# Rolling an 8192 x 8192 array by 100 columns: heads through SBUF, or unaligned pieces straight from HBM to HBM

## The chip, the cores and the metric

The kernel runs on one core of a Trainium2 chip. The metric is the device time of one execution in microseconds; the figure is the median of several runs. Array rows are 8192 float32 values, so a row is 32,768 bytes, and a column is 4 bytes. Input and output both lie in HBM, 268.4 MB each.

## The reference

```python
def setup_inputs():
    return {
        "x": np.random.randn(8192, 8192).astype(np.float32),
        "shift": 100,
    }

def reference(x: np.ndarray, shift: int) -> np.ndarray:
    return np.roll(x, shift, axis=1)
```

Nothing is calculated. Each row of the output is the same row of the input moved right by s = 100 columns, and the last 100 columns of the input become the first 100 of the output (the wrapped end, 400 bytes a row).

## The kernel before

The kernel cuts each output row at column a. For s = 100 the first two lines below make a = 256, so the cut is at byte 1024 of the row.

```python
s = shift % n_cols
a = -(-s // 128) * 128
if 0 < a <= 384 and a + 128 <= n_cols:
    a += 128
g = a - s                      # 156
engines = [nc.sync, nc.scalar]
```

**The long pieces**, output columns 256 to 8191, come from input columns 156 to 8091. They are copied straight from HBM to HBM. A block is 64 rows; each of its four DMAs takes 16 rows (every fourth one), and the DMAs alternate between the queues of SP (`nc.sync`) and ACT (`nc.scalar`). In the last four of the 128 blocks every DMA is cut into two halves of the row.

```python
xm = x.rearrange("(c e j) w -> c j e w", e=16, j=4)
om = out.rearrange("(c e j) w -> c j e w", e=16, j=4)
blocks = n_rows // 64
mid = (a + n_cols) // 256 * 128
for c in range(blocks):
    parts = ((a, mid), (mid, n_cols)) if c >= blocks - 4 and a < mid else ((a, n_cols),)
    for j in range(4):
        for lo, hi in parts:
            engines[j % 2].dma_start(out=om[c, j, :, lo:hi], in_=xm[c, j, :, lo - s:hi - s])
```

**The heads**, output columns 0 to 255, consist of the wrapped end (100 columns) and the first 156 columns of the input row. They go through SBUF on GpSimd's own queue, in four stages of 2048 rows. For three rows of four one load reads 256 columns that begin 100 columns ahead of the row's start in memory, so that the end of the row above and the start of this row come as one piece; the vector engine copies the two parts to their rows in the tile `h`. Then four stores for each stage write 1024 bytes a row.

```python
Q, J = 4, 4
n_st = n_rows // (P * Q * J)                       # 4 stages
for k in range(n_st):
    t = reads.tile([P, Q - 1, J, a], x.dtype)
    h = heads.tile([P, Q, J, a], x.dtype)
    for q in range(1, Q):
        lead = bass.AP(tensor=x.tensor, offset=(k * P * J * Q + q) * n_cols - s, ...)
        nc.gpsimd.dma_start(out=t[:, q - 1], in_=lead)
    nc.gpsimd.dma_start(out=h[:, Q - 1, :, :s], in_=xt[k, Q - 1, :, :, n_cols - s:])
    nc.vector.tensor_copy(h[:, :Q - 1, :, :s], t[:, :, :, :s])
    if g > 0:
        nc.gpsimd.dma_start(out=h[:, 0, :, s:], in_=xt[k, 0, :, :, :g])
        nc.vector.tensor_copy(h[:, 1:, :, s:], t[:, :, :, s:])
    tiles.append(h)
for k, h in enumerate(tiles):
    for q in range(Q):
        nc.gpsimd.dma_start(out=ot[k, q, :, :, :a], in_=h[:, q])
```

Of the kernel before, what the change touches and what calls it, by code (L numbers as in the profile page):

```python
# [1 line left out]

# [4 lines left out]


@with_exitstack
def kernel(  # L10
    ctx: ExitStack,
    tc: tile.TileContext,
    x: bass.AP,
    shift: int,
    out: bass.AP,
):
    nc = tc.nc
    n_rows, n_cols = x.shape
    s = shift % n_cols
    a = -(-s // 128) * 128  # L20
    if 0 < a <= 384 and a + 128 <= n_cols:
        a += 128
    g = a - s
    P = nc.NUM_PARTITIONS
    engines = [nc.sync, nc.scalar]
    n_chunks = 16
    rows = n_rows // n_chunks

    xm = x.rearrange("(c e j) w -> c j e w", e=16, j=4)
    om = out.rearrange("(c e j) w -> c j e w", e=16, j=4)
    if a < n_cols:
        blocks = n_rows // 64
        mid = (a + n_cols) // 256 * 128
        for c in range(blocks):
            parts = ((a, mid), (mid, n_cols)) if c >= blocks - 4 and a < mid else ((a, n_cols),)  # L40
            for j in range(4):
                for lo, hi in parts:
                    engines[j % 2].dma_start(out=om[c, j, :, lo:hi], in_=xm[c, j, :, lo - s:hi - s])
    if a == 0:
        return


    if a > 512:
        for i in range(n_chunks):
            r = slice(i * rows, (i + 1) * rows)  # L50
            nc.gpsimd.dma_start(out=out[r, :s], in_=x[r, n_cols - s:])
            if g > 0:
                nc.gpsimd.dma_start(out=out[r, s:a], in_=x[r, :g])
        return

    Q, J = 4, 4  # L60
    n_st = n_rows // (P * Q * J)
    reads = ctx.enter_context(tc.tile_pool(name="reads", bufs=n_st))
    heads = ctx.enter_context(tc.tile_pool(name="heads", bufs=n_st))
    xt = x.rearrange("(k p j q) c -> k q p j c", q=Q, j=J, p=P)
    ot = out.rearrange("(k p j q) c -> k q p j c", q=Q, j=J, p=P)
    tiles = []
    for k in range(n_st):
        t = reads.tile([P, Q - 1, J, a], x.dtype)
        h = heads.tile([P, Q, J, a], x.dtype)
        for q in range(1, Q):  # L70
            lead = bass.AP(tensor=x.tensor, offset=(k * P * J * Q + q) * n_cols - s,
                           ap=[[J * Q * n_cols, P], [Q * n_cols, J], [1, a]])
            nc.gpsimd.dma_start(out=t[:, q - 1], in_=lead)  # L73
        nc.gpsimd.dma_start(out=h[:, Q - 1, :, :s], in_=xt[k, Q - 1, :, :, n_cols - s:])  # L74
        nc.vector.tensor_copy(h[:, :Q - 1, :, :s], t[:, :, :, :s])  # L75
        if g > 0:
            nc.gpsimd.dma_start(out=h[:, 0, :, s:], in_=xt[k, 0, :, :, :g])  # L77
            nc.vector.tensor_copy(h[:, 1:, :, s:], t[:, :, :, s:])  # L78
        tiles.append(h)
    for k, h in enumerate(tiles):  # L80
        for q in range(Q):
            nc.gpsimd.dma_start(out=ot[k, q, :, :, :a], in_=h[:, q])  # L82


# [1 line left out]
_INS = ['x', 'shift']  # L86
_OUTS = [((8192, 8192), 'float32')]

_NUMBERS = {'shift': 100}


# [26 lines left out]
```

## Time and profile before

| | |
|---|---|
| time, median of 3 | 829.27 us (829.12 to 830.45) |
| span of the profiled execution | 817.9 us |
| DMAs of long pieces | 496 of 496 KB, 32 of 248 KB |
| DMAs of heads on GpSimd's queue | 20 loads, 16 stores |
| vector engine, GpSimd busy | 7.7 us, 28.9 us |

Of the long pieces there are 248 DMAs of 496 KB on each of the two queues and, in the last four blocks, 16 of 248 KB on each. Among the profile's DMA queues q1 and q10 carry the long pieces of the two issuing engines, and q0 carries the heads. The MB of a queue count each packet once: a piece that goes from HBM to HBM is one packet, though it is read from HBM and written to it, and a head is two, one into SBUF and one out of it. A queue's share is the time its packets took out of the time of all 16 DMA engines. Besides data packets there are packets of 4 bytes that tell of a finished transfer; they take almost no time but are counted. The row "DMA" gives the busy share of the engines in 40 slices of the span, in tenths.

### The profile page before, as it was taken

What the parts mean: (1) busy time and instruction counts of PE and PEld (TensorE: products, weight loads), DVE (VectorE), ACT (ScalarE), POOL (GpSimd) and SP (SyncE); (2) the same over time, 40 slices, a digit from 0 to 9 for tenths busy, and PEclk for the clock granted to TensorE, in tenths of its full rate; (3) what the DMA queues carried; (4) which work ended last, traced back from release to release, by engine and by line L of the source; (5) the groups of instructions that cost most, each with busy time, mean ns of one, the idle gap of its engine ahead of it and who ended that gap; (6) DMA issues with size and microseconds to landing.
All of it is one profiled execution on the core that took longest, in us unless ns stands there. A gap on an engine that the chain in (4) does not pass through costs nothing. (4 is left out here: it accounts for less than half of the span.)

```text
span 817.9 us, 633 instructions
## 1 busy us (share of the span) xinstructions
DVE 7.7 (1%) x8; POOL 28.9 (4%) x40
## 2 busy tenths in 40 slices
DVE  0000000000000000000000000000000000000000
POOL 3000000010010000000000000000000000000000
DMA  9999999999999999999999999999999999999998
GB/s 307 333 348 342 347 355 347 355 356 344 350 338 363 359 351 354 361 346 360 334 333 341 326 335 331 331 332 337 328 338 331 330 336 331 335 334 326 331 308 299
DMA packets 21572, 276.89 MB, mean 339 GB/s; under 512 B 9024, under 2 KB 9024, under 8 KB 13120
## 3 DMA queue, kind: packets, MB, share of 16 engines
q10 hardware_dynamic: 8448, 130.04, 46.5%
q1 hardware_dynamic: 8448, 130.04, 45.9%
q0 software_dynamic: 4672, 16.78, 6.9%
q14 instruction: 4, 0.03, 0.0%
HBM read 268.44 MB, written 268.44 MB: 656 GB/s over the span
## 5 line engine op out<-in xcount | busy, mean ns | idle before, releaser
L82 POOL DMA_DIRECT2D out_dram<-h x16 | 13.2, 827 | 196.6 <-DMA out_dram<-h 112.1
L73 POOL DMA_DIRECT2D t<-in_x_dram x12 | 9.5, 795 | 60.4 <-DMA h<-in_x_dram 30.1
L75 DVE COPY h<-t 128x1200 f32<-128x1200 f32 x4 | 3.1, 785 | 233.6 <-DMA t<-in_x_dram 233.6
L78 DVE COPY h<-t 128x1872 f32<-128x1872 f32 x4 | 4.9, 1224 | 0.0
L74 POOL DMA_DIRECT2D h<-in_x_dram x4 | 3.0, 749 | 45.6 <-DMA t<-in_x_dram 45.6
L77 POOL DMA_DIRECT2D h<-in_x_dram x4 | 3.0, 751 | 42.8 <-DMA t<-in_x_dram 42.8
L99 POOL MEMSET const-float32-0.0<- 128x1 f32 x1 | 0.1, 100 | 0.2 <-issue 0.2
L99 POOL MEMSET const-bfloat16-1.0<- 128x1 bf16 x1 | 0.1, 103 | 0.0
L99 POOL MEMSET const-float32-1.0<- 128x1 f32 x1 | 0.1, 100 | 0.0
L99 POOL MEMSET const-uint8-127<- 128x1 uint8 x1 | 0.1, 100 | 0.0
## 6 DMA issues: line engine op xcount, KB each, us to landing
out_dram<-in_x_dram ACTq DMA_DIRECT2D x248, 496.0 KB, 12.7
out_dram<-in_x_dram SPq DMA_DIRECT2D x248, 496.0 KB, 12.7
out_dram<-h POOLq DMA_DIRECT2D x16, 512.0 KB, 112.6
t<-in_x_dram POOLq DMA_DIRECT2D x12, 512.0 KB, 95.4
out_dram<-in_x_dram SPq DMA_DIRECT2D x16, 248.0 KB, 5.7
out_dram<-in_x_dram ACTq DMA_DIRECT2D x16, 248.0 KB, 5.9
h<-in_x_dram POOLq DMA_DIRECT2D x4, 312.0 KB, 92.0
h<-in_x_dram POOLq DMA_DIRECT2D x4, 200.0 KB, 97.9
```

The costliest lines, as they stand in the source:

```text
L73: nc.gpsimd.dma_start(out=t[:, q - 1], in_=lead)
L74: nc.gpsimd.dma_start(out=h[:, Q - 1, :, :s], in_=xt[k, Q - 1, :, :, n_cols - s:])
L75: nc.vector.tensor_copy(h[:, :Q - 1, :, :s], t[:, :, :, :s])
L77: nc.gpsimd.dma_start(out=h[:, 0, :, s:], in_=xt[k, 0, :, :, :g])
L78: nc.vector.tensor_copy(h[:, 1:, :, s:], t[:, :, :, s:])
L82: nc.gpsimd.dma_start(out=ot[k, q, :, :, :a], in_=h[:, q])
L99: nc = _bacc.Bacc("TRN2", target_bir_lowering=False, num_devices=1)
```

## The change

The new kernel does away with the heads' detour. The long pieces start where the roll makes them start, at output column 100 (byte 400) and input column 0, and run to the row's end, 8092 columns or 32,368 bytes. The wrapped ends, 100 columns or 400 bytes a row, are copied from HBM to HBM as well, by one DMA for each block of 64 rows on ACT's queue, after the block's four long pieces. The last blocks are not cut in half. GpSimd, the vector engine and SBUF have no part in it any more. It is for a simpler path: all of the array is moved by the two hardware queues, with no second transfer and no waiting on tiles.

```diff
-    a = -(-s // 128) * 128
-    if 0 < a <= 384 and a + 128 <= n_cols:
-        a += 128
-    g = a - s
...
-    if a < n_cols:
-        blocks = n_rows // 64
-        mid = (a + n_cols) // 256 * 128
-        for c in range(blocks):
-            parts = ((a, mid), (mid, n_cols)) if c >= blocks - 4 and a < mid else ((a, n_cols),)
-            for j in range(4):
-                for lo, hi in parts:
-                    engines[j % 2].dma_start(out=om[c, j, :, lo:hi], in_=xm[c, j, :, lo - s:hi - s])
...
-    (heads: all loads, copies and stores shown above)
...
+    blocks = n_rows // 64
+    xb = x.rearrange("(c e j) w -> c j e w", e=16, j=4)
+    ob = out.rearrange("(c e j) w -> c j e w", e=16, j=4)
+    xw = x.rearrange("(c e j) w -> c e j w", e=16, j=4)
+    ow = out.rearrange("(c e j) w -> c e j w", e=16, j=4)
...
+    tail = 0
+    for c in range(blocks - tail):
+        for j in range(4):
+            engines[j % 2].dma_start(out=ob[c, j, :, s:], in_=xb[c, j, :, :n_cols - s])
+        if s > 0:
+            engines[1].dma_start(out=ow[c, :, :, :s], in_=xw[c, :, :, n_cols - s:])
+    if tail:
...                            (not reached: tail is 0)
```

More of the change, by code (lines that the diff above doesn't have):

```diff
@@ L19 @@
     s = shift % n_cols
-    a = -(-s // 128) * 128
-    if 0 < a <= 384 and a + 128 <= n_cols:
-        a += 128
-    g = a - s
-    P = nc.NUM_PARTITIONS
-    engines = [nc.sync, nc.scalar]
[L26 to L35, printed above, removed]
-    if a < n_cols:
-        blocks = n_rows // 64
-        mid = (a + n_cols) // 256 * 128
-        for c in range(blocks):
-            parts = ((a, mid), (mid, n_cols)) if c >= blocks - 4 and a < mid else ((a, n_cols),)
-            for j in range(4):
-                for lo, hi in parts:
-                    engines[j % 2].dma_start(out=om[c, j, :, lo:hi], in_=xm[c, j, :, lo - s:hi - s])
@@ L44 @@
[L44 to L79, printed above, removed]
@@ L80 @@
-    for k, h in enumerate(tiles):
-        for q in range(Q):
-            nc.gpsimd.dma_start(out=ot[k, q, :, :, :a], in_=h[:, q])
+    engines = [nc.sync, nc.scalar]
+    blocks = n_rows // 64
[3 more added lines that the diff above has]
+    ow = out.rearrange("(c e j) w -> c e j w", e=16, j=4)
+    xt = x.rearrange("(t c e j) w -> t j e c w", c=4, e=16, j=4)
+    ot = out.rearrange("(t c e j) w -> t j e c w", c=4, e=16, j=4)
@@ new lines @@
+    tail = 0
[5 more added lines that the diff above has]
+    if tail:
+        t = blocks // 4 - 1
+        if s > 0:
+            for c in range(blocks - tail, blocks):
+                engines[c % 2].dma_start(out=ow[c, :, :, :s], in_=xw[c, :, :, n_cols - s:])
+        for j in range(4):
+            engines[j % 2].dma_start(out=ot[t, j, :, :, s:], in_=xt[t, j, :, :, :n_cols - s])
```

## Prediction

> **What bounds the kernel now.** I read the page first: the DMA row and the byte counts, because no engine computes for more than 4% of the span.
>
> ```profile
> span 817.9 us, 633 instructions
> DVE 7.7 (1%) x8; POOL 28.9 (4%) x40
> ...
> DMA  9999999999999999999999999999999999999998
> ...
> q10 hardware_dynamic: 8448, 130.04, 46.5%
> q1 hardware_dynamic: 8448, 130.04, 45.9%
> q0 software_dynamic: 4672, 16.78, 6.9%
> ...
> HBM read 268.44 MB, written 268.44 MB: 656 GB/s over the span
> ```
>
> The 16 DMA engines are busy in every slice, and the three queues fill 46.5 + 45.9 + 6.9 = 99.3% of their time. HBM traffic is the least possible: the array is read once and written once. So the time is bytes over rate, plus a start and an end, and the question is what sets the rate. For that I compared two stretches of the DMA view: 40 to 300 us, where GpSimd's queue q0 runs beside the long pieces, and 380 to 780 us, where the long pieces run almost alone.
>
> ```profile
> q10 hardware_dynamic: 2520, 40.03, 43.1%
> q1 hardware_dynamic: 2517, 39.94, 42.2%
> q0 software_dynamic: 3107, 11.09, 15.0%
> ```
>
> ```profile
> q10 hardware_dynamic: 4160, 65.97, 50.2%
> q1 hardware_dynamic: 4165, 66.13, 48.9%
> q0 software_dynamic: 363, 1.31, 0.9%
> ```
>
> The columns are packets, MB and share of the engines' time. In the second stretch 132.1 MB of long pieces took 99.1% of 16 engines for 400 us, 6342 us of engine time: 20.8 bytes per ns, or 1.52 us for a row of 31,744 bytes. In the first, 79.97 MB took 85.3% of 16 x 260 us = 3548 us: 22.5 bytes per ns, 1.41 us for the same row. The same row is 8% faster when the engines also have SBUF work. So an engine's own speed isn't the limit. Now HBM traffic: a long piece is read from and written to HBM, a packet of q0 touches HBM once. First stretch: (2 x 79.97 + 11.09) MB in 260 us = 658 GB/s. Second: (2 x 132.1 + 1.31) in 400 us = 664 GB/s. The HBM traffic is nearly constant (1% apart) while the mix of work changes by 15 points. **My reading is that HBM traffic bounds the kernel at about 664 GB/s**, and that the SBUF detour of the heads costs only that 1% over the stretch in which it runs.
>
> Then the waits of the issuing queues and the end of the span:
>
> ```profile
> SPq L43 <- DMA out_dram<-in_x_dram: 671.1, 259, 3.9
> ```
>
> ```profile
> out_dram<-in_x_dram ACTq DMA_DIRECT2D x248, 496.0 KB, 12.7
> out_dram<-in_x_dram SPq DMA_DIRECT2D x248, 496.0 KB, 12.7
> ```
>
> ```profile
> 780.00:800.00 20.00, 0.00 (x0) 0.00 (x0) 1.00 0.89 299
> 800.00:818.00 18.00, 0.00 (x0) 0.00 (x0) 1.00 0.84 295
> ```
>
> SP issues 264 long pieces and waits for an earlier one before 259 of them. An issue takes 0.51 us, a transfer lands 12.7 us after it, and in 380 to 780 us each queue issued 131, one in 3.05 us. So 12.7 / 3.05, about four, are in flight on each queue, eight in all. The issuing engines are far from being the limit. The last fence (DMA share and GB/s are its last columns) is the stage with half rows: 16 DMAs of 248 KB on each queue. There the engines were busy for 0.89 and 0.84 and moved about 297 GB/s against 333. Over 38 us that is a loss of 38 x (1 - 297/333), about 4 us.
>
> [...] The wrapped ends are 400 B. No HBM write that short exists in the kernel before, so its trace can't say; 400 B pieces are only read there, into SBUF. [...] The long pieces before have an unaligned source (column 156, byte 624) and an aligned destination (byte 1024), and run at the rate above. After, it is the other way round: source byte 0, destination byte 400. [...]
>
> **The change, part by part.**
>
> Long pieces. 8192 rows of 8092 x 4 = 32,368 B, 265.2 MB instead of 260.0. With the heads, all 268.4 MB goes HBM to HBM. At the rate of the second stretch, (132.1 + 0.66) MB in 400 us or 332 GB/s of copying (q0's one-sided MB count half), this is 268.4 / 0.332 = 808 us. The page's own start costs little: the first 20 us ran at 304 GB/s, a loss of about 2 us.
>
> Removed: GpSimd's 36 DMAs and the DVE's 8 copies. DVE and POOL lie wholly beside the transfers, so their 7.7 and 28.9 us bring nothing. q0's HBM traffic isn't removed, it only moves. What is gained is the 1% (658 to 664) over the 380 us in which q0 was active: 380 x 0.9% = 3.4 us. That gain is already in the 808.
>
> Added: 128 head DMAs of 64 x 400 B. Each engine gets 4 pieces per DMA, 512 in all. Their bytes at 20.8 per ns are 19 ns a piece and are counted in the 808. What such a piece costs over its bytes isn't in this profile; I choose 20 to 60 ns as a guess, so 10 to 31 us of engine time. As HBM is the limit, most of this is hidden: before, q0 took 15% of engine time, of which about half was HBM-free, and the HBM rate fell by 1%, so some seven eighths of a loss of HBM demand was made up by the other engines. An eighth of 10 to 31 us is 1 to 4 us. [...] I take 6 us for the heads.
>
> ACT issues 256 + 128 DMAs of 0.52 us, 199 us of some 815: beside the path. The heads also take places among the eight in flight. A block is now four long pieces and one head, so of eight 6.4 are long: 6.4 x 1.55 is some 10 us of work queued on each engine instead of 12.4. With half rows it was some 6 us, and there the engines ran dry for 11 to 16%; at 10 us I expect hardly any of that, 1 us.
>
> The end. The stage of half rows, with its 4 us, goes. In its place the last whole rows drain with less evenness over engines: one row is 1.55 us, and a few rows of difference between engines would leave a similar 4 us.
>
> Sum of the span: 808 + 2 (start) + 6 (heads) + 1 (places in flight) + 4 (end), 821 us, against 817.9. The times of before lie 829.27 - 817.9 = 11.4 us above the span; I keep that: 832 us. As I hold both the 6 us and the end for cautious, I set the point at **830 us**: the change moves almost nothing, because HBM traffic stays as it was.
>
> **Rivals.**
>
> A. *Unaligned writes cost.* [...] A cost of 5% on the rate alone would give 830 + 40 = 870 us, and it could be more. For it: the kernel takes pains to start its long pieces at a multiple of 512 B and to write heads of 1024 B. Against: the same misalignment is there now on the read side[...]. I give it about one chance in six.
>
> B. *Short pieces block the engines.* [...] 100 ns or more a piece is 51 us of engine time, and if it is not hidden the time goes to some 850 to 870 us. For it: [...] the detour through SBUF, which avoids such pieces. [...]
>
> C. *Aligned reads help.* If the unaligned source now costs extra traffic and an unaligned destination does not, the rate rises by a few per cent: 800 to 812 us. For it: nothing in the profile[...]. One chance in twelve.
>
> D. *Heads are free and the end is smooth*: 808 + 2 + 3 + 11.4, about 824 us. This is the lower half of my range.
>
> **Range and chances.** A gain over 2% needs under 812.7 us, thus a span under 801 us and a copying rate above that of the quiet stretch; only C gives it: 0.09. A loss over 2% is above 845.9 us, which A or B bring: 0.29. Between lies 0.62. The range is 815 to 858 us: the lower end lies between C and D, the upper is a moderate A or B.
>
> **What would show it.** Right: in the changed profile HBM read and written stay at 268.44 MB, no q0 data, the copying rate in the middle is 328 to 336 GB/s, a long row takes 1.5 to 1.6 us of engine time, and a long piece lands in about 10 us. The heads' packets would take under 5% of the engines. A is right if long packets take clearly longer per byte than 1 / 20.8 ns with the DMA row full. B is right if the long ones keep their rate, ACT's queue takes clearly more time than SP's, or DMA shares fall. Slices below 0.95 in the middle would show that 6.4 places in flight are too few. I'd be wrong altogether if the bound isn't HBM traffic but a limit on each engine's packets: then fewer packets of q0 would show as a gain that I don't count.

## The result and the profile after

The kernel after takes **834.65 us** (median of 7), beside 829.42 us for the kernel before in the same runs: ratio **1.005, 95% interval 1.003 to 1.007**. The change is a small loss, clear of the noise. The prediction was 830 us, with a range of 815 to 858 us.

The page of the kernel after, the lines that answer to those shown of before:

```profile
span 829.0 us, 685 instructions
...
DMA  9999999999999999999999999999999999999998
GB/s 302 326 321 323 330 328 329 329 318 329 319 330 318 332 323 332 324 325 329 327 320 327 331 328 325 324 329 321 326 321 330 317 325 328 327 329 323 327 322 285
...
q10 hardware_dynamic: 18432, 135.88, 51.0%
q1 hardware_dynamic: 8192, 132.60, 48.2%
...
HBM read 268.44 MB, written 268.44 MB: 648 GB/s over the span
```

The engines are as full as before. The line of HBM bytes says less than the prediction hoped for. It gives 268,435,456 bytes each way, the size of the array to the byte, and for the kernel without heads (experiment 5) 265.16 MB, which is what its DMAs name. On these pages the line gives the bytes that the DMAs name; no run shows whether traffic beyond those would appear in it. q0 has gone. ACT's queue has 18,432 packets: 4096 long rows, 8192 heads and 6144 finish marks of 4 bytes, 16 for each of its 384 DMAs. So each 400 B piece is a packet of its own. A finish mark takes 9 ns in the mean; all 10,240 of both queues fill 5.8 us of an engine in the mean of the 16, 0.7% of the span. In the packet records the 8192 heads take 14.8 us of an engine in the mean, 1.8% of the span, which is most of the difference between 51.0% and 48.2%.

The first profile of before, span 817.9 us, is of an execution quicker than the timed ones. The kernel before, profiled again beside its timing runs, has a span of 826.4 us (experiment 1). Here is its DMA view from 380 to 780 us, then that of after (packets, MB, share of 16 engines; for the issues KB each and us to landing):

```profile
q10 hardware_dynamic: 4114, 65.31, 49.9%
q1 hardware_dynamic: 4117, 65.40, 48.9%
q0 software_dynamic: 480, 1.72, 1.1%
```

```profile
q10 hardware_dynamic: 8866, 65.39, 50.9%
q1 hardware_dynamic: 4007, 64.81, 48.8%
...
out_dram<-in_x_dram SPq DMA_DIRECT2D x126, 505.8 KB, 8.6
out_dram<-in_x_dram ACTq DMA_DIRECT2D x123, 505.8 KB, 10.8
out_dram<-in_x_dram ACTq DMA_DIRECT2D x62, 25.0 KB, 12.1
```

HBM traffic before: (2 x 130.71 + 1.72) MB in 400 us, 658 GB/s. After: 2 x 130.20 in 400 us, 651 GB/s. That is a rate 1% lower in the middle. From 40 to 300 us, where the detour was at work, the same views give 650 before and 652 after: there the new kernel is no slower. A queue's wait after:

```profile
SPq L31 <- DMA out_dram<-in_x_dram: 669.8, 207, 9.0
```

The longest single wait rose from 3.9 to 9.0 us. ACT's queue carries the heads as well, and SP's transfers land sooner (8.6 us against 10.8); that SP therefore runs ahead and waits longer is likely, but was not tested. It is no loss by itself: the DMA share stays at 0.99 to 1.01 from 40 to 780 us.

### The profile page after: what moved, and what is told of

Its sections match the earlier page's. It is cut to its first block, busy times and chain, and to the rows that moved or that the text cites. A ratio compares the mean times of both kernels' runs of the same rounds, so it can differ in the third digit from the quotient of the medians.

```text
span 829.0 us, 685 instructions
## 1 busy us (share of the span) xinstructions
POOL 0.2 (0%) x4
## 2 busy tenths in 40 slices
DMA packets 26629, 268.52 MB, mean 324 GB/s; under 512 B 18432, under 2 KB 18432, under 8 KB 18432
## 3 DMA queue, kind: packets, MB, share of 16 engines
q10 hardware_dynamic: 18432, 135.88, 51.0%
q1 hardware_dynamic: 8192, 132.60, 48.2%
HBM read 268.44 MB, written 268.44 MB: 648 GB/s over the span
## 6 DMA issues: line engine op xcount, KB each, us to landing
out_dram<-in_x_dram ACTq DMA_DIRECT2D x128, 25.0 KB, 12.1
```

## The experiments

Ratios are to the kernel before in the same set of runs. Four sets were run: experiments 1 to 4, 5 to 8, 9 to 11, and 12. They ran on different chips (numbers 4, 10, 11 and 10), and the kernel before took 829.3, 827.8, 819.4 and 829.4 us in them. So times of different sets are not compared, only ratios, on the assumption that a ratio carries over from chip to chip. Experiments 2 and 5 support it: 8064 columns took 0.9848 on chip 4, and by bytes 8092 columns should take 0.9882; on chip 10 they took 0.9886.

In the expectations, theory 1 is the prediction's reading that HBM traffic sets the time, theory 2 its rival A (unaligned writes cost), and theory B its rival B (each short piece holds an engine up). The 5% of rival A and the 100 ns a piece of rival B were suppositions of the author, not taken from a trace.

**1. The kernel before, once more** (no edit).

> The kernel before, unchanged, to have a span and a time of the same execution. The span of the first profile was 817.9 us while the executions took 829.4 in the median; after, span and time of one execution lie 1.8 us apart. If the first profile was just an unusually quick execution, this span is 825 to 830 us and time less span is about 2 us; the quiet stretch 380 to 780 us then shows 655 to 660 GB/s of HBM traffic instead of 664. If profile and time differ by a constant 11 us for this kernel, the span is again about 818.

Measured: 829.99 us, ratio 1.0001 (0.9986 to 1.0016). Span and time of the profiled execution: 826.4 and 828.55 us. Time is span plus some 2 us; the 11.4 us between the first profile and the timed runs was not a constant of the kernel. The spans of this kernel on chips 4 and 10 lie between 823.5 and 830.7 us, those on chip 11 between 815.8 and 820.3. Of these three the first profile's 817.9 us fits chip 11 alone; on which chip it was taken is not known.

**2 to 4. Alignment by itself.** The long pieces alone, 8064 columns, heads left out (the values of d and r for the first of the three). An offset is called aligned here if it is a multiple of 512 bytes, as the cuts of the kernel before are:

```diff
+    d, r, n = 100, 0, 8064
...
-            engines[j % 2].dma_start(out=ob[c, j, :, s:], in_=xb[c, j, :, :n_cols - s])
+            engines[j % 2].dma_start(out=ob[c, j, :, d:d + n], in_=xb[c, j, :, r:r + n])
-        if s > 0:
-            engines[1].dma_start(out=ow[c, :, :, :s], in_=xw[c, :, :, n_cols - s:])
```

With d = 100, r = 0 (destination unaligned):

> Only the long pieces, 8064 columns from input column 0 to output column 100 (destination unaligned, source aligned); the other 128 columns of a row are left out. Theory 1 (HBM traffic alone): 264.2 MB at the rate of the kernel after, about 815 to 820 us, and the same as the next two kernels within 0.5%. Theory 2 (unaligned writes cost): slower than the one with an aligned destination by over 1%.

With d = 128, r = 28 (source unaligned):

> The same 8064 columns, from input column 28 to output column 128: destination aligned to 512 bytes, source unaligned, the way of the kernel before; 128 columns left out. Theory 1: the same time as the one from column 0 to column 100 within 0.5%. Theory 2: faster than it by 1% or more. Theory 3 (unaligned reads cost): slower than it.

With d = r = 128 (both aligned, nothing shifted):

> The same 8064 columns, from input column 128 to output column 128: both aligned, so nothing is shifted; 128 columns left out. Theory 1: the same time as the other two within 0.5%. If alignment of either side costs, this is the fastest of the three, by the sum of both costs.

| destination, source | us | ratio, interval |
|---|---|---|
| byte 400, byte 0 | 818.33 | 0.9848, 0.9825 to 0.9871 |
| byte 512, byte 112 | 813.82 | 0.9799, 0.9776 to 0.9823 |
| byte 512, byte 512 | 810.08 | 0.9756, 0.9734 to 0.9778 |

Same bytes, same DMAs, and the executions of the three do not overlap (816.60 to 819.05, 812.37 to 815.82, 809.77 to 811.67 us). The unaligned source costs 3.7 us over the aligned copy, the unaligned destination 8.3 us. So turning the one into the other, as the change does, costs 4.5 us, 0.5%. Theory 1 in the form "only bytes count" misses this; theory 2 has the right sign, but its size (over 1%) is not reached; theory 3, that the kernel with the unaligned source is the slower of the two, falls. One offset of each kind was tried. The third kernel shifts nothing, so against it the distance between source and destination changes too; the 4.5 us between the first two is free of that, as both shift by 100 columns.

**5. The kernel after without heads.** Output columns 0 to 99 are left out:

```diff
-        if s > 0:
-            engines[1].dma_start(out=ow[c, :, :, :s], in_=xw[c, :, :, n_cols - s:])
```

> The kernel after without its 128 head DMAs: all else as it is, the first 100 columns of the output are left out. Its bytes are 3.28 MB fewer, about 10.0 us at the 326 GB/s of the middle of the kernel after. Theory 1 (heads cost their bytes and a few us more): 834.65 less 10 less 2 to 6, thus 819 to 823 us. Theory B (short pieces block the engines, 100 ns each): below 800 us. The two long-piece kernels that are known, 818.3 us for 8064 columns, speak for 821.

Measured: 817.9 us, ratio 0.9886 (0.9868 to 0.9904). The heads cost 1.005 - 0.9886 = 1.6% or about 13.6 us, with some 2 us of uncertainty. Their bytes are 10.0 us of it. Some 3.6 us, with the same 2 us of uncertainty, are left for their being short. Theory B, 100 ns a piece, falls. In the packet records an engine spends, in the mean of the 16, 802 us on long pieces and 14.8 us on heads in the kernel after, and 804 us on long pieces here: of the 14.8 us of the heads' packets 13.6 are paid.

**6. Half the HBM traffic.** The same long pieces, read from 128 rows in SBUF; the output is those rows over and over, heads left out:

```diff
+    pool = ctx.enter_context(tc.tile_pool(name="src", bufs=1))
+    src = pool.tile([128, n_cols], x.dtype)
+    nc.sync.dma_start(out=src[:], in_=x[0:128, :])
+    sv = src.rearrange("(e k) w -> k e w", k=8)
...
-            engines[j % 2].dma_start(out=ob[c, j, :, s:], in_=xb[c, j, :, :n_cols - s])
+            engines[j % 2].dma_start(out=ob[c, j, :, s:], in_=sv[(4 * c + j) % 8, :, :n_cols - s])
```

> The same long pieces of 32,368 bytes in the same DMAs on the same queues, but read from 128 rows held in SBUF instead of from HBM; heads left out, and the output holds the same 128 rows again and again. HBM is only written, so its traffic is halved while each DMA engine moves the same number of packets and bytes. Theory 1 (HBM traffic is the limit): the rate goes from 327 GB/s to that of the shortest long packet, 32,368 bytes in 1196 ns or 433 GB/s: a span near 615 to 650 us. Rival (each DMA engine is limited by its packets or by what it holds in flight, whatever HBM has to carry): 800 to 820 us, as without heads.

Measured: 692.26 us, ratio 0.837 (0.8353 to 0.8388). The view by stretches (start and end, length, POOL, clock, DMA share, GB/s):

```profile
40.00:100.00 60.00, 0.00 (x0) 1.00 1.00 276
100.00:160.00 60.00, 0.00 (x0) 1.00 1.00 331
160.00:220.00 60.00, 0.00 (x0) 1.00 1.00 414
220.00:400.00 180.00, 0.00 (x0) 1.00 1.01 429
400.00:640.00 240.00, 0.00 (x0) 1.00 1.00 423
```

From 220 us on the same engines, with packets of the same size in the same DMAs, carry 423 to 429 GB/s instead of the 327 of experiment 5. So the engines' own speed is not the limit of the copy from HBM to HBM; the limit lies on the side of HBM. The run doesn't tell HBM's bandwidth from the delay of its reads, as both are away, and reads of HBM alone were not run. One thing speaks against a fixed delay in each engine: in the packet records a long row of the kernel before takes 1.53 us in the mean when the heads are left out (experiment 8) and 1.48 us when they are there (experiment 1), although the heads then share the engines.

The total lies outside both expected ranges, because the first stretch is slow: 276 GB/s of writes alone, less than half of the 651 GB/s of HBM traffic in the kernel after, with the DMA share at 1.00. The amount of traffic can't explain that.

**7. Twice as many head pieces.** Same bytes and number of head DMAs, pieces of 200 B:

```diff
+    xh = x.rearrange("(d e j) w -> d e j w", e=16, j=8)
+    oh = out.rearrange("(d e j) w -> d e j w", e=16, j=8)
...
-        if s > 0:
-            engines[1].dma_start(out=ow[c, :, :, :s], in_=xw[c, :, :, n_cols - s:])
+        lo = c % 2 * (s // 2)
+        hi = lo + s // 2
+        engines[1].dma_start(out=oh[c // 2, :, :, lo:hi], in_=xh[c // 2, :, :, n_cols - s + lo:n_cols - s + hi])
```

> The kernel after, its heads in pieces of 200 bytes: 128 head DMAs as before, each with 128 rows and one half of the 100 columns, so the same bytes in twice as many pieces. Theory 1 (cost by bytes, the rest mostly hidden): 834 to 838 us. Theory B (cost by piece): the heads' cost above their bytes doubles; with 100 ns a piece that is 50 us more, with the 29 ns of a 400 B packet that the trace after shows at most 10 us more.

Measured: 840.59 us, ratio 1.0149 (1.0125 to 1.0172): 1% or some 8 us over the kernel after, with 2 to 3 us of uncertainty. The 834 to 838 of theory 1 is missed, and so is theory B with 100 ns a piece (50 us); the "at most 10 us" from the packets' own time holds. In the packet records a 400 B packet takes 24 ns in the median and 29 in the mean, a 200 B packet 16 and 19. For each of the 16 engines there are 512 packets of 29 ns after and 1024 of 19 ns here, so the packets themselves account for 4.6 us of the 8; the rest is at the edge of the uncertainty and not explained. At equal bytes, heads cost more when there are more of them.

**8. The kernel before without heads.** Only its long pieces, with half rows at the end; columns 0 to 255 are left out:

```diff
-    tiles = []
-    for k in range(n_st):
-        ...                        (all of the heads)
```

> The kernel before without its heads: only the long pieces, output columns 256 to 8191 with half rows in the last blocks; the first 256 columns are left out. Theory 1: 260.0 MB at 329 GB/s is 790 us, with 2 us of start and 4 of end 797 us; the detour through SBUF then costs 829.4 less 797, about 32 us for 16.8 MB of HBM traffic, of which 25 us are its bytes. If the detour were nearly as cheap as its HBM traffic alone: 804 us. If it took all its engine share (6.9% of 818, 56 us): 773 us.

Measured: 797.44 us, ratio 0.964 (0.962 to 0.9659). The detour costs 827.82 - 797.44 = 30.4 us, with some 2 us of uncertainty, as theory 1 said; 25.5 of them are the bytes at 329 GB/s. GpSimd's queue filled 6.9% of the engines' time, 56 us; little more than half of it is paid. The middle of the two kernels without heads, first this one, then experiment 5:

```profile
380.00:680.00 300.00, 0.00 (x0) 1.00 1.00 330
```

```profile
380.00:680.00 300.00, 0.00 (x0) 1.00 1.00 327
```

The last column, GB/s, differs by 0.7% before rounding (98.88 MB against 98.17), with the DMA share at 1.00 in both. That is near the 0.5% of alignment in experiments 2 to 4; the rows differ a little in length, too.

**9. The half rows put back** into the kernel after:

```diff
+    mid = n_cols // 2
...
+        parts = ((s, mid), (mid, n_cols)) if c >= blocks - 4 else ((s, n_cols),)
         for j in range(4):
-            engines[j % 2].dma_start(out=ob[c, j, :, s:], in_=xb[c, j, :, :n_cols - s])
+            for lo, hi in parts:
+                engines[j % 2].dma_start(out=ob[c, j, :, lo:hi], in_=xb[c, j, :, lo - s:hi - s])
```

> The kernel after with the long pieces of its last four blocks in halves again, as before had them. If the missing half rows cost something at the end, this gains 1 to 4 us over the kernel after (ratio 1.000 to 1.004 against 1.005); by the prediction, which put 4 us for either end, nothing changes (1.005).

Measured: ratio 1.006 (1.0047 to 1.0073), against 1.005 without them. The intervals overlap; half rows make no difference that these runs show. The ends by stretches, the kernel after first, then this one:

```profile
800.00:815.00 15.00, 0.00 (x0) 1.00 1.01 326
815.00:829.00 14.00, 0.00 (x0) 1.00 0.80 263
```

```profile
780.00:800.00 20.00, 0.00 (x0) 1.00 0.97 326
800.00:824.00 24.00, 0.00 (x0) 1.00 0.80 266
```

With whole rows the rate holds until 14 us before the end and then falls to 263; with half rows it is 266 over the last 24 us. Against 326 that is a loss of 14 x (1 - 263/326), about 3 us, and of 24 x (1 - 266/326), about 4 us.

**10. Heads issued by GpSimd**, whose DMAs the profile shows on a queue of their own (q0):

```diff
-        if s > 0:
-            engines[1].dma_start(out=ow[c, :, :, :s], in_=xw[c, :, :, n_cols - s:])
+        nc.gpsimd.dma_start(out=ow[c, :, :, :s], in_=xw[c, :, :, n_cols - s:])
```

> The kernel after with its head DMAs issued by GpSimd instead of ACT, the same pieces in the same order. They then take no place among the eight transfers of SP and ACT, and in the kernel before packets of GpSimd's queue joined ten or so 400 B pieces (4000 to 4400 bytes in some 160 to 170 ns, 16 ns a piece against 24 ns of a single 400 B packet after). Theory 1 (bytes): same as after, within 3 us (1.002 to 1.007). Rival (places in flight or the single packets cost what the heads cost above their bytes): 3 to 4 us less, about 1.000 to 1.001.

Measured: ratio 1.0027 (1.0013 to 1.0041), some 2 us better than on ACT, though the intervals overlap (1.003 to 1.007 on ACT). It falls inside the band given for theory 1 and short of the rival's. Its page has the heads in 2048 data packets of 1600 bytes:

```profile
q0 software_dynamic: 4096, 3.28, 2.2%
```

Here the queue joined four pieces to a packet (4096 packets less 2048 finish marks). In the kernel before it did the same with the heads on their way through SBUF: 16.78 MB in 4096 data packets, 4096 bytes each in the mean, so a head was not a packet of its own there. From 380 to 680 us 193 long pieces were issued, which land after 12.5 us: some eight of them in flight, by an estimate of 193 x 12.5 / 300. In the kernel after the view from 380 to 780 us gives, in the same way, some six ((126 x 8.6 + 123 x 10.8) / 400) and two heads (62 x 12.1 / 400). Whether the gain is from the two places or from the joined pieces isn't told apart. It is still no better than the kernel before.

**11. The kernel before, cut at column 128**: heads of 512 B through SBUF.

```diff
-    if 0 < a <= 384 and a + 128 <= n_cols:
-        a += 128
```

> The kernel before with the cut at column 128 instead of 256: heads of 512 bytes through SBUF, long pieces still aligned to 512 bytes and longer. The head detour carries half the HBM traffic. If what the detour costs above its bytes (30.4 less 25.5, about 5 us in the kernel before) goes with its bytes, this gains 2 to 3 us: ratio 0.997. If it goes with the number of pieces, which stays, the ratio is 1.000; if 512 B stores or 112 B loads are dear, over 1.003.

Measured: ratio 1.0041 (1.0026 to 1.0055), slower, as in the last of the three cases expected. The same long pieces alone, destination aligned and source at byte 112, stand at 0.9799 (experiment 3), so these heads cost 2.4%, 20 us, for 8.39 MB of HBM traffic whose bytes take 12.7 us at 330 GB/s: 7 us above the bytes, with 2 us of uncertainty, no less than the 4.9 us with pieces of 1024 B. Half the bytes in as many pieces do not halve the surplus. Which of the loads and stores it comes from was not tried.

**12. Neighbouring rows.** As experiment 10, but a long DMA takes 16 rows 32 KB apart instead of 128 KB:

```diff
-    xb = x.rearrange("(c e j) w -> c j e w", e=16, j=4)
-    ob = out.rearrange("(c e j) w -> c j e w", e=16, j=4)
+    xb = x.rearrange("(c j e) w -> c j e w", e=16, j=4)
+    ob = out.rearrange("(c j e) w -> c j e w", e=16, j=4)
```

> The kernel with head DMAs on GpSimd, its long pieces taken by 16 rows that follow each other (32 KB apart) instead of every fourth row (128 KB apart). Theory 1 in its plain form (the limit is the amount of HBM traffic, whatever the addresses): ratio 1.0027 as with every fourth row, within 0.002. Rival (the limit is how the rows that are under way together fall on HBM, which the slow first quarter of the writes from SBUF, 218 to 345 GB/s, suggests): a change of 1% or more, to either side; if it's faster by 0.5% it beats both kernels.

Measured: ratio 1.0202 (1.0172 to 1.0233), 1.7% slower than experiment 10 by their ratios, with the same bytes, packets and queues. By stretches, the middle of experiment 10 first, then this one:

```profile
380.00:680.00 300.00, 1.51 (x3) 1.00 1.00 332
```

```profile
40.00:240.00 200.00, 29.82 (x59) 1.00 0.99 316
240.00:440.00 200.00, 26.27 (x52) 1.00 0.99 320
440.00:640.00 200.00, 0.00 (x0) 1.00 1.00 324
```

The engines are full (DMA share 0.99 to 1.00), and the rate is lower and rises slowly (experiment 10 has 329, 330 and 332 in the same three stretches). So the limit is not the amount of HBM traffic alone; which rows are under way counts too. The edit changes both which 16 rows go together and which follow one another in the same place of a DMA, and these are not told apart. Theory 1 in its plain form falls here; that the limit lies on the side of HBM stays.

## Why the prediction was right, and where it was not

**The bound.** That something on HBM's side, not the engines' packets, sets the rate held (experiment 6), and so did its first consequence, that replacing one path by another of the same HBM traffic moves little. "HBM traffic bounds the kernel at about 664 GB/s" was too simple: with the bytes fixed, alignment moved the time by up to 1% (experiments 2 to 4) and the order of rows by 1.7% (experiment 12), and in the first 160 us of experiment 6 much less traffic brought at most 331 GB/s. Of the signs named in advance, the copying rate in the middle missed its range (326 GB/s, not 328 to 336), and the HBM byte count is no sign at all: it is the size of the array before and after.

**Span against time: this step failed.** "The times of before lie 829.27 - 817.9 = 11.4 us above the span; I keep that." The distance is 2 us. The sum of 821 us was thus a sum for an execution as quick as the profiled one and has to be compared with its 817.9: a ratio of 1.004, where 1.005 was measured. Adding 11.4 us happened to do the same, as it put the slower level of the timed runs in: luck. The last step, from 832 down to 830 because two terms were held "for cautious", went the wrong way.

**The detour removed.** Put at 3.4 us above its bytes, measured 4.9, with 2 us of uncertainty. Right.

**The heads.** Put at 10 us of bytes and 6 above; measured 10.0 and 3.6. The size is near, but the steps to it were not right. The guess of 20 to 60 ns over the bytes of a piece was too high: a packet takes 24 ns in the median and 29 in the mean, 5 to 10 more than the 19 for its bytes. That "most of this is hidden" did not hold either: of the 14.8 us that heads fill on each engine 13.6 are paid, or above the bytes 3.6 of some 5, with 2 us of uncertainty, where an eighth was expected. A cost set too high times a share set too low came out near. What lay between the estimate of 1 to 4 us and the 6 us of the sum rested on nothing measured; all that the 400 B pieces pay for being short is some 3.6 us.

**Alignment: the step that left it out.** The sum had no term for it, and rival A came with 5% and one chance in six. The term exists and is 4.5 us, a tenth of rival A. The first half of rival C, that unaligned reads cost, is true too, with 3.7 us, but the change pays more for the write than it gets back for the read. The reason given against A, that the same misalignment is there on the read side, was thus half right: both sides cost, and at the offsets tried writing costs twice as much.

**Places in flight.** A landing of about 10 us was expected: 8.6 and 10.8 us on the two queues. The engines did not run dry (DMA share 0.99 to 1.01 from 40 to 780 us); experiment 10 leaves some 2 us, and as much uncertainty, for this and the single packets together.

**The end.** 4 us was expected with half rows and without: the rates give about 4 and 3, and the times show no difference (experiment 9). Right.

**The sum from the runs:** less 30.4 us for the detour; 156 columns more in the long pieces, 5.11 MB or 15.6 us; 4.5 us for alignment; 13.6 us for the heads. That is +3.3 us, ratio 1.004. The first and the last term are differences to the two kernels themselves, so what the sum tests is its middle: 15.6 + 4.5 = 20.1 us, where 817.9 - 797.44 = 20.5 us was measured between experiments 8 and 5. What is gained by dropping the detour (4.9 us above its bytes) is less than what goes to the heads' shortness (3.6) and to the unaligned writes (4.5), each known to some 2 us. So the prediction's small sum came out because its errors nearly cancelled: it lacked 4.5 us for alignment, and it had some 5 us too much: 3.4 in the heads with their places in flight (7 against 3.6), and 1.5 in the detour (a gain of 3.4 against 4.9).

No variant tried beats the kernel before. The bytes alone, at the rate of its own long pieces, would take 797.44 x 268.44 / 260.05 = 823 us, ratio 0.994 to its 827.82: at that rate there was never more than about half a per cent to win.

## What to carry to other kernels

When the DMA row is full, ask whether the engines or HBM are the limit: compare two stretches with a different mix of work, and see which rate stays put (here the engines' moved by 8%, HBM's by 1%). Dropping a path for another that carries the same bytes gave back here only what the first cost above those bytes, 4.9 us of 829; a kernel with the part in question left out measures that directly. And take span and time from one and the same execution before carrying a difference between them.

## What was not expected of the hardware

Writes from SBUF to HBM began at 276 GB/s with the DMA share at 1.00 (40 to 100 us) and reached 429 only after some 200 us, in one and the same loop; why is open. Copying 16 neighbouring rows at a time (32 KB apart) was 1.7% slower than every fourth row (128 KB apart), ratio 1.0202 against 1.0027. A copy of rows of 32,256 bytes from HBM to HBM took 810.08 us with source and destination at byte 512 of the row, 813.82 us (0.5% more) with the source at byte 112, and 818.33 us (1.0% more) from byte 0 to byte 400. And one kernel took 1.2% less on chip 11 (819.4 us) than on chip 4 (829.3 us), more than the change that was to be measured.
